# Groups of products kept together in TensorE's program

## The chip, the cores and the metric

The kernel runs on one core of a Trainium2 chip. The metric is the device time of one execution in microseconds; the median of 3 runs of the kernel before is 1662.76 us (1661.94 to 1663.72).

## The reference: what is computed

One inference step through two layers, for 128 context tokens and 256 latent tokens of width 2048, in fp32. Each layer starts with an RMSNorm that is shifted and scaled by a modulation vector, `silu(cond) @ mod_w + mod_b`, a product of a vector with a 2048 x 6144 matrix for each of two conditions (`c` for the latent, `c_ctx` for the context tokens).

- Layer 0: `proj = h @ w_in` (2048 x 6400). Part of it goes into a bidirectional RWKV-7 recurrence with 16 heads of 64, `s = s * w - (s @ kk) kka + v k`, `o = s @ r`, over each token sequence and in both directions; another part through `real(fft2)` over tokens and channels. Both are gated by `silu` of a further part, and multiplied by a 2048 x 2048 output matrix.
- Layer 1: grouped-query attention, 32 query heads on 8 key heads of 64, over a window of 128 and 128 cached context keys, with a sink logit per head in the softmax; a `silu` gate and a second output matrix.
- After each layer: RMSNorm, a gate from the modulation, and the residual.

It returns the tokens, the recurrence's final context states, and the context keys and values of layer 1.

## The kernel before

**Large products.** Activations and weights are split into a rounded high part and the rest (`hhi`, `hlo`; `whi`, `wlo`, made by ScalarE at L258 and VectorE at L259), and each product of a 128-row block is three products of the one-pass type (mm3, L398 to L400). proj_cm gives accumulators with channels in partitions and 384 tokens in columns; proj_tm with tokens in partitions. Weights come as units of 128 x 512, loaded by SyncE's queue into 2 and later 4 buffers, and cast up to 2 or 3 units ahead (Stream).

**Small products** are fp32, and the profile shows each as two records. A unit of the modulation vector (mod_unit, L322) is four products, one for each block of 128 weight rows, whose outputs of 32 rows each go to the four quarters of one accumulator, ps_mod. Their raw weights come in three ways: `mraw` at the start (blocks that layer 0 needs first), `rawf` in a lane of the RWKV stage (FILL_MODS, 7 blocks in halves of 256 columns, one buffer), and `raw` in the weight stream during the gates and the first output projection (PE_MODS, 2 blocks of 512 columns, four units each). Other blocks are summed by VectorE (mod_sums, L345).

The recurrence is done in chunks of 64 tokens. For one chunk of a pair of heads: ps_ba (L1026) and ps_sc (L1046) are products of keys and queries within chunks, ps_z (L1101, L1111) part of solving a triangular system, ps_v (L1149) transposes values, and the chain from chunk to chunk has ps_p1 (L1168), ps_y (L1176), ps_o (L1188 and L1208) and ps_s (L1195). They take half the array's rows, half its columns, or both, and the two heads `h` of a pair lie in different halves. In attention, `scores` makes the logits of two heads (L1479 to L1485), transpose_p transposes the softmax (L1515 to L1521), and ps_pv (L1442, L1444) multiplies it with the values, again with two heads in the two halves of the array's columns.

**What sets the order.** The code is traced lane by lane: weave asks, by a planner's costs in each `yield`, which lane goes on, and the traced instructions are numbered. The number is the priority: it counts up, and LEAD, BOOST and BACK shift it for some lanes and steps. A scheduler then puts each engine's program in a fixed order: of the instructions that are ready it takes the one with the lowest number. So a product that is traced right behind another one can come later in TensorE's program, with other lanes' products between. At run time an engine takes its program in order.

Of the kernel before, what the change touches and what calls it, by code (L numbers as in the profile page):

```python
# [20 lines left out]
KT = 16  # L21
TP, TS = 128, 256
# [14 lines left out]

BACK = 120
# [265 lines left out]
class K:  # L304
    def __init__(self, tc, A):
        self.tc, self.nc, self.A = tc, tc.nc, A


    def mod_unit(self, raw, layer, b, u, dst, c0=0):
# [10 lines left out]
        for i in range(4):  # L320
            kt = 4 * u + i
            nc.tensor.matmul(acc[32 * i:32 * i + 32, :n], self.silu[:, 2 * kt:2 * kt + 32], raw[:, n * i:n * i + n],  # L322
                             start=(u == 0), stop=(u == 3), skip_group_check=True)
# [6 lines left out]
        for m in range(nm):  # L330
            nc.tensor.matmul(ps[:, 2 * m:2 * m + 2], rows[:, 128 * m:128 * m + 128], self.sel, start=True, stop=True)
# [5 lines left out]
    def mod_sums(self, raw, i, layer, b, u):  # L337
# [12 lines left out]
        for g in range(4):  # L350
            nc.tensor.matmul(ps[32 * g:32 * g + 32, 0:8], self.sel32, self.dacc[:, :, g], start=True, stop=True)
# [43 lines left out]

    def mm3(self, out, lh, ll, rh, rl, start, stop):
        mm = self.nc.tensor.matmul
# [186 lines left out]
    def layer0_in(self, acts, first):  # L584
# [32 lines left out]
        for kt in range(KT):  # L617
            sq = ip.tile([128, T], F32, name="sq", tag="sq", bufs=2)
            nc.scalar.activation(sq, xT[:, kt], AF.Square)
            nc.tensor.matmul(ps[:, :T], ones, sq, start=(kt == 0), stop=(kt == KT - 1))  # L620
# [192 lines left out]
    def dft(self, fp, ch, dt, us, ys, y):  # L813
# [8 lines left out]
        for tt in range(3):  # L822
            ps = self.pw.tile([128, 512], F32, name="ps_f1", tag="pw")
            ts = slice(128 * tt, 128 * tt + 128)
            nc.tensor.matmul(ps[:, 0:129], us[0][:, ts], ch[:, 0:129], start=True, stop=False)
            nc.tensor.matmul(ps[:, 65:129], us[1][:, ts], ch[:, 129:193], start=False, stop=False)
            nc.tensor.matmul(ps[:, 129:257], us[1][:, ts], ch[:, 193:321], start=False, stop=True)
            nc.scalar.copy(ab[:, tt], ps[:, 0:257])
# [5 lines left out]
        for out, c0, n, q in ((ps[:, 0:194], 1, 128, 0), (ps[:, 194:388], 129, 128, 1), (px[0:1, 0:194], 0, 1, 0)):  # L834
            for tt in range(3):
                nc.tensor.matmul(out[:, cols[tt]], ab[:, tt, c0:c0 + n], tabs[tt][q],
                                 start=(tt == 0 and c0 != 129), stop=(tt == 2 and c0 != 1))
# [63 lines left out]
    def wkv_elem(self, j, st):  # L901
# [25 lines left out]
        nc.tensor.matmul(ps[:, :T], self.bd, sq, start=True, stop=True)  # L927
# [7 lines left out]
        for q, src, dst in ((0, self.wl, p), (1, self.al, tha)):  # L935
            yield 0.92, 0, 1.8
            ps = [self.pw.tile([128, 512], F32, name="ps_lo", tag="pw") for _ in range(2)]
            for d in range(2):
                nc.tensor.matmul(ps[d][:, :T], up[64 * d:64 * d + 64, q], src[64 * d:64 * d + 64, :],
# [39 lines left out]
        nc.tensor.matmul(ps[:, :T], self.bd, sq, start=True, stop=True)  # L979
# [30 lines left out]
    def wkv_lower(self, j, st):  # L1010
# [4 lines left out]
        for v0s in ((8, 0), (4,)):  # L1015
# [6 lines left out]
            for i in range(n):  # L1022
                v = v0s[i // 4] + i % 4
                for h in range(2):
                    hs = slice(64 * h, 64 * h + 64)
                    nc.tensor.matmul(ps[hs, 64 * i:64 * i + 64], BK[hs, v, 0], A[hs, v], start=True, stop=True)  # L1026
# [6 lines left out]
    def wkv_score(self, j, st):  # L1033
# [3 lines left out]
        for v0 in (8, 0, 4):  # L1037
# [4 lines left out]
            for i in range(4):  # L1042
                for h in range(2):
                    hs = slice(64 * h, 64 * h + 64)
                    lh = BK[hs, v0 + i].rearrange("p a t -> p (a t)")
                    nc.tensor.matmul(ps[h][:, 128 * i:128 * i + 128], lh, AR[hs, :, v0 + i], start=True, stop=True)  # L1046
# [8 lines left out]
        for v0, n in ((0, 4), (4, 2), (8, 4)):  # L1055
            yield 0.22 * n, 0, 0.9
            ps = self.pw.tile([128, 512], F32, name="ps_bt", tag="pw")
            for i in range(n):
                nc.tensor.transpose(ps[:, 128 * i:128 * i + 128], BK[:, v0 + i].rearrange("p a t -> p (a t)"),
                                    self.ident)  # L1060
# [3 lines left out]
    def wkv_solve(self, p):  # L1064
# [31 lines left out]
        for u0, n in ((0, 16), (16, 8)):  # L1096
            yield 0.06 * n, 0, 0.5
            ps = self.pw.tile([128, 512], F32, name="ps_z", tag="pw")
            for u in range(n):
                for h in range(2):  # L1100
                    nc.tensor.matmul(ps[quad[2 * h + 1], 32 * u:32 * u + 32], TI[quad[2 * h], u0 + u, 32:64],  # L1101
                                     R[quad[2 * h], u0 + u, :], start=True, stop=True)
# [3 lines left out]
        for u0, n in ((0, 16), (16, 8)):  # L1106
            yield 0.06 * n, 0, 0.9
            ps = self.pw.tile([128, 512], F32, name="ps_z2", tag="pw")
            for u in range(n):
                for h in range(2):  # L1110
                    nc.tensor.matmul(ps[quad[2 * h], 32 * u:32 * u + 32], Z[quad[2 * h + 1], u0 + u, :],  # L1111
                                     DB[quad[2 * h + 1], u0 + u, :], start=True, stop=True)
# [5 lines left out]
    def wkv_chain(self, j, st):  # L1118

        nc, kp = self.nc, self.kp  # L1120
        TT, mm = nc.vector.tensor_tensor, nc.tensor.matmul
# [22 lines left out]
        def values(c):  # L1144

            ps = self.pw.tile([128, 512], F32, name="ps_v", tag="pw")
            for slot, s, d, _ in units(c):
                w0 = 64 * c + (TP if s == 0 else 0)
                mm(ps[64:128, 128 * slot:128 * slot + 128], (vrev if d else v)[:, w0:w0 + 64], self.ident,  # L1149
                   start=True, stop=True)  # L1150
# [10 lines left out]
        for c in range(4):  # L1161
# [4 lines left out]
            for slot, s, d, v_ in un:  # L1166
                for h in range(2):
                    mm(p1[64 * h:64 * h + 64, 64 * slot:64 * slot + 64], SC[:, 12 * h + v_, 0:64],  # L1168
                       SV[:, h, slot, :], start=True, stop=True)
# [3 lines left out]
            for slot, s, d, v_ in un:  # L1173
                for h in range(2):
                    hs, sl = slice(64 * h, 64 * h + 64), slice(64 * slot, 64 * slot + 64)
                    mm(yps[hs, sl], TI[hs, self.pos(v_)], P1[hs, sl], start=True, stop=True)  # L1176
# [8 lines left out]
            for slot, s, d, v_ in un:  # L1185
                for h in range(2):
                    hs, sl = slice(64 * h, 64 * h + 64), slice(64 * slot, 64 * slot + 64)
                    mm(ops[hs, sl], SB[hs, slot], R[hs, v_], start=(slot == 0), stop=False, skip_group_check=True)  # L1188
            if c < 3:
                yield 0.13 * ns, 0.7, 2.2  # L1190
                sps = self.pw.tile([128, 512], F32, name="ps_s", tag="pw")
                for slot, s, d, v_ in un:
                    for h in range(2):
                        q = (h * ns + slot) * 64
                        mm(sps[0:64, q:q + 64], BT[:, v_ - 2 * s, 64 * h:64 * h + 64], UV[:, h, slot, :],  # L1195
                           start=True, stop=True)
# [8 lines left out]
            for slot, s, d, v_ in un:  # L1205
                sl = slice(64 * slot, 64 * slot + 64)
                for h in range(2):
                    mm(ops[64 * h:64 * h + 64, sl], UV[:, h, slot, :], SC[:, 12 * h + v_, 64:128],  # L1208
                       start=False, stop=(slot == ns - 1), skip_group_check=True)
# [19 lines left out]
    def wkv_norm(self, j, st):  # L1229
# [6 lines left out]
        nc.tensor.matmul(ps[:, :T], self.bd, o, start=True, stop=True)  # L1236
# [5 lines left out]
        nc.tensor.matmul(ps[:, :T], self.bd, s2, start=True, stop=True)  # L1242
# [8 lines left out]
    def out_proj(self, layer, ys):  # L1251
# [10 lines left out]
        for b in range(4):  # L1262
# [3 lines left out]
            for m in range(4):  # L1266
                nc.tensor.matmul(ps[0:2, 128 * m:128 * m + 128], mc[:, g0 + b, m], self.ident, start=True, stop=True)
# [53 lines left out]
        if layer == 0:  # L1321
# [6 lines left out]
            for kt in range(KT):  # L1328
                ps = self.pw.tile([128, 512], F32, name="ps_t", tag="pw")
                for tt in range(3):  # L1330
                    nc.tensor.transpose(ps[:, 128 * tt:128 * tt + 128], xr[:, tt, 128 * kt:128 * kt + 128], self.ident)
# [12 lines left out]
    def layer1_mix(self, acts):  # L1344
# [78 lines left out]
        def heads(b):  # L1423
            for i in range(2):
# [13 lines left out]
                for kt in range(-1, 3):  # L1438
                    for hh in range(2):
                        hr = slice(64 * hh, 64 * hh + 64)  # L1440
                        if kt < 0:
                            nc.tensor.matmul(pv[hr, 0:TP], vp[:, gs], ps[hh][:, 768:896], start=True, stop=False)  # L1442
                        else:
                            nc.tensor.matmul(pv[hr, TP:T], vs[:, kt, gs], ps[hh][:, 256 * kt:256 * kt + 256],  # L1444
                                             start=False, stop=(kt == 2))
# [22 lines left out]
    def scores(self, qs, kh, kl, cmask):  # L1468
# [3 lines left out]
        mm = self.nc.tensor.matmul  # L1472
# [4 lines left out]
        for q, s in zip(qs, out):  # L1477
            for n, sc, qc, kc in jobs:
                mm(s[n][:, sc], q[:, qc], kh[:, kc], start=(sc.start == 0), stop=False)  # L1479
            mm(s[0][:, 128:256], cmask[:, 0:128], cmask[:, 128:256], start=False, stop=False)  # L1480
            mm(s[1][:, 0:128], cmask[:, 0:128], cmask[:, 256:384], start=False, stop=False)
        for j, (n, sc, qc, kc) in enumerate(jobs):
            for hh, (q, s) in enumerate(zip(qs, out)):
                hr = slice(64 * hh, 64 * hh + 64)
                mm(s[n][:, sc], q[hr, qc], kl[hr, kc], start=False, stop=(j > 0))  # L1485
# [23 lines left out]
    def transpose_p(self, ap, p):  # L1509
# [3 lines left out]
        for kt in range(2):  # L1513
            for qb in range(2):
                nc.tensor.transpose(ta[:, 256 * kt + 128 * qb:256 * kt + 128 * qb + 128],  # L1515
                                    p[qb][:, 128 * kt:128 * kt + 128], self.ident)
        nc.scalar.copy(PT[:, 0:512], ta)
        tb = self.pw.tile([128, 512], F32, name="ps_tb", tag="pw")
        for qb in range(2):
            nc.tensor.transpose(tb[:, 128 * qb:128 * qb + 128], p[qb][:, 256:384], self.ident)  # L1520
        nc.tensor.transpose(tb[:, 256:384], p[2], self.ident)  # L1521
# [19 lines left out]
```

## Time and profile before

| | before |
|---|---|
| median of 3 runs | 1662.76 us |
| the profiled execution | 1660.11 us, of which its span 1658.3 us |
| busy TensorE / VectorE / ScalarE | 1570.1 / 1072.3 / 811.3 us |
| mean granted TensorE clock | 0.979 |
| the large products into acc, L398 / L399 / L400, 1376 each | busy 479.6 / 473.9 / 473.6 us |
| ps_mod (L322), records, and busy: rawf, mraw, raw | 448, 256, 64; 53.0, 35.9, 28.2 us |
| chain that ended last: TensorE, VectorE, DMA, ScalarE | 72, 11, 9, 5% |

Busy is the time in which at least one instruction of a group ran; products overlap each other in TensorE, so durations of single ones add up to more. The stages along the span, as the lines that run in them show: modulation and first norm to about 130 us, RWKV to 640 us, Fourier mixing and gates to 895 us, the first output projection to 1035 us, the second norm and keys and values to 1110 us, attention to 1400 us, then its gates and the second output projection.

### The profile page before, as it was taken

To read this page: it belongs to the slowest core of one execution; us is meant where nothing else is said; L and a number is where in the kernel's file an instruction comes from. 1 tells how busy PE (TensorE), PEld (TensorE's weight loads), DVE (VectorE), ACT (ScalarE), POOL (GpSimd) and SP (SyncE) were. 2 spreads that over 40 slices of the span, in tenths; PEclk is the share of its full clock that TensorE was granted. 3 is DMA by queue.
4 is the path that set the end of the run, shared out by engine and by line. 5 is a ranking of instruction groups with operands and counts; after the bars stand their busy time and mean duration, and the time that the engine had idled before them with its cause. 6 is when DMAs were issued, how large, how long until landed. Compare 5 with 4: busy or idle time off the path is not lost.

```text
span 1658.3 us, 30019 instructions
## 1 busy us (share of the span) xinstructions
PE 1570.1 (95%) x11488; PEld 1296.5 (78%) x11488; DVE 1072.3 (65%) x2584; ACT 811.3 (49%) x1771; POOL 3.9 (0%) x21
## 2 busy tenths in 40 slices
PE   6899999999989989999999999899999999999998
PEld 2557678777777768889897777788888888998777
DVE  1326886587777585475664573899877999644344
ACT  3326656665667654354333333754555555333332
POOL 0000000000000000000000000000000000000000
PEclk8899999999999999999999999899999999999999
DMA  9975342253233243354456663567322334446443
GB/s 368 370 279 167 115 143 74 86 162 121 79 118 111 76 132 94 109 168 121 156 184 231 245 209 120 198 187 248 107 72 69 102 127 148 131 121 226 132 126 134
DMA packets 120247, 255.75 MB, mean 154 GB/s; under 512 B 12324, under 2 KB 45220, under 8 KB 109732
## 3 DMA queue, kind: packets, MB, share of 16 engines
q1 hardware_dynamic: 111528, 235.97, 43.3%
q10 hardware_dynamic: 8576, 17.86, 3.1%
q8 instruction: 90, 1.47, 0.4%
q14 instruction: 53, 0.43, 0.1%
HBM read 246.40 MB, written 7.39 MB: 153 GB/s over the span
## 4 chain that ended last, share of the span: by engine, by line
PE 72%; DVE 11%; DMA 9%; ACT 5%; issue 2%; ACTq 0%; SPq 0%; DVEq 0%
PE acc L398 11%; PE acc L399 11%; PE acc L400 11%; PE ps_mod L322 6%; DMA rawf<-modw 6%; PE acct L398 5%; PE acct L399 5%; PE acct L400 5%; DVE wlo L259 2%; DMA raw<-we 2%; DVE junk L345 1%; PE ps_pv L1444 1%; PE ps_v L1149 1%; PE ps_s L1195 1%; PE ps_y L1176 1%
## 5 line engine op out<-in xcount | busy, mean ns | idle before, releaser
L258 ACT CAST whi<-raw 128x512 fp32r<-128x512 f32 x480 | 295.5, 620 | 477.3 <-PE acc L399 207.6
L259 DVE TENSOR_TENSOR wlo<-raw,whi 128x512 fp32r<-128x512 f32 x480 | 327.9, 689 | 304.4 <-ACT whi L258 301.3
L398 PE MATMUL acc<-hhi,whi 128*128 128x384 f32 x1376 | 479.6, 349 | 13.9 <-ACT whi L258 7.2
L400 PE MATMUL acc<-hhi,wlo 128*128 128x384 f32 x1376 | 473.6, 345 | 0.8 <-DVE wlo L259 0.5
L399 PE MATMUL acc<-hlo,whi 128*128 128x384 f32 x1376 | 473.9, 344 | 0.0
L398 PEld LDWEIGHTS acc<-hhi,whi 128*128 128x128 f32 x1376 | 261.9, 190 | 48.9 <-issue 19.9
L399 PEld LDWEIGHTS acc<-hlo,whi 128*128 128x128 f32 x1376 | 262.6, 191 | 16.8 <-issue 15.4
L400 PEld LDWEIGHTS acc<-hhi,wlo 128*128 128x128 f32 x1376 | 262.0, 190 | 14.2 <-issue 9.6
L345 DVE SCALAR_TENSOR_TENSOR junk<-raw,srow 128x512 f32<-128x512 f32 x224 | 154.2, 688 | 5.8 <-DMA raw<-modw 2.4
L398 PE MATMUL acct<-whi,yhi 128*128 128x512 f32 (+1 forms) x432 | 154.8, 360 | 1.2 <-DVE yb L1276 0.9
L399 PE MATMUL acct<-wlo,yhi 128*128 128x512 f32 (+1 forms) x432 | 154.7, 358 | 0.8 <-DVE wlo L259 0.8
L400 PE MATMUL acct<-whi,ylo 128*128 128x512 f32 (+1 forms) x432 | 154.3, 358 | 0.0
L398 PEld LDWEIGHTS acct<-whi,yhi 128*128 128x128 f32 x432 | 81.5, 189 | 21.6 <-DVE yb L1276 5.3
L399 PEld LDWEIGHTS acct<-wlo,yhi 128*128 128x128 f32 x432 | 81.5, 189 | 17.4 <-issue 4.2
L400 PEld LDWEIGHTS acct<-whi,ylo 128*128 128x128 f32 x432 | 81.5, 189 | 16.5 <-issue 4.4
L322 PE MATMUL ps_mod<-rawf,silu 128*32 128x256 f32 x448 | 53.0, 404 | 23.1 <-DMA rawf<-modw 23.1
L322 PE MATMUL ps_mod<-mraw,silu 128*32 128x512 f32 x256 | 35.9, 667 | 10.9 <-DMA mraw<-modw 10.9
L322 PEld LDWEIGHTS ps_mod<-rawf,silu 128*32 128x32 f32 x448 | 12.4, 109 | 41.5 <-DMA rawf<-modw 25.4
L327 ACT COPY mrow<-ps_mod 128x256 f32<-128x256 f32 (+1 forms) x24 | 11.1, 461 | 63.1 <-PE ps_mod L322 63.1
L1086 DVE TENSOR_TENSOR work<-work 128x30 f32<-128x30 f32 (+14 forms) x120 | 39.3, 328 | 1.9
L1084 DVE TENSOR_TENSOR work<-work 128x30 f32<-128x30 f32 (+14 forms) x120 | 39.3, 327 | 1.9
L1494 DVE TENSOR_REDUCE ast<-ps_sa 128x1 f32<-128x384 f32 x64 | 25.4, 416 | 19.2 <-PE ps_sa L1485 19.1
(298 smaller groups left out, 2169.8 us busy)
## 6 DMA issues: line engine op xcount, KB each, us to landing
raw<-we SPq DMA_DIRECT2D x200, 256.0 KB, 2.8
raw<-wo SPq DMA_DIRECT2D x160, 256.0 KB, 2.7
raw<-modw SPq DMA_DIRECT2D x36, 1024.0 KB, 5.7
mraw<-modw SPq DMA_DIRECT2D x32, 1024.0 KB, 8.2
rawf<-modw SPq DMA_DIRECT2D x56, 512.0 KB, 3.9
raw<-weo SPq DMA_DIRECT2D x64, 256.0 KB, 2.8
raw<-woo SPq DMA_DIRECT2D x64, 256.0 KB, 2.7
G<-gd ACTq DMA_DIRECT2D x4, 1024.0 KB, 6.9
```

Source lines behind the costliest of these rows:

```text
L258: k.nc.scalar.copy(hi, raw)
L259: k.nc.vector.tensor_tensor(lo, raw, hi, op=ALU.subtract)
L322: nc.tensor.matmul(acc[32 * i:32 * i + 32, :n], self.silu[:, 2 * kt:2 * kt + 32], raw[:, n * i:n * i + n], start=(u == 0), stop=(u == 3), ...
L345: nc.vector.scalar_tensor_tensor(junk, raw[:, 512 * i:512 * i + 512], 1.0, self.srow[:, c], op0=ALU.mult, op1=ALU.mult, accum_out=self.dac ...
L398: mm(out, lh, rh, start=start, stop=False)
L399: mm(out, lh, rl, start=False, stop=False)
L400: mm(out, ll, rh, start=False, stop=stop)
L1084: TT(tv, X[:, s + 1:32, s:s + 1].to_broadcast([128, n, s]), X[:, s:s + 1, 0:s].to_broadcast([128, n, s]), op=ALU.mult)
L1086: TT(X[:, s + 1:32, 0:s], X[:, s + 1:32, 0:s], tv, op=ALU.add)
L1149: mm(ps[64:128, 128 * slot:128 * slot + 128], (vrev if d else v)[:, w0:w0 + 64], self.ident, start=True, stop=True)
L1176: mm(yps[hs, sl], TI[hs, self.pos(v_)], P1[hs, sl], start=True, stop=True)
L1494: nc.vector.tensor_reduce(st[:, 0, i:i + 1], src[i], axis=AX.X, op=ALU.max)
```

## The change

Inside `with self.together():` the first product that is traced is the head. Each later one of the block gets an order edge that puts it behind the head (`issue_after`, an edge without a semaphore), and a priority that is better by 1,000,000. Every product goes through `mm` or `tp`; outside such a block these do what the direct calls did. The blocks are: a unit of ps_mod, ps_mt, the first Fourier products, ps_ba, ps_sc, ps_bt, ps_z, ps_v, ps_p1, ps_y, both halves of ps_o, ps_s, ps_pv, the scores of two heads, and each of the two groups of transposes. In some, the order within the block is changed too: ps_o, ps_s and ps_pv start with head h = 1, ps_sc counts down, ps_ba runs through the indices as `x ^ 3`, ps_ta and ps_tb start with another block.

```
+NEXT = 1000000
+    def on_pe(self, op, args, kw):
+        if self.head is None:
+            op(*args, **kw)
+        elif not self.head:
+            self.head.append(op(*args, **kw).ins)
+        else:
+            with self.tc.issue_after(self.head[0]):
+                self.tc.cur_priority -= NEXT
+                op(*args, **kw)
+                self.tc.cur_priority += NEXT
+
+    def mm(self, *args, **kw):
+        self.on_pe(self.nc.tensor.matmul, args, kw)
+
+    def tp(self, *args, **kw):
+        self.on_pe(self.nc.tensor.transpose, args, kw)
+
+    @contextmanager
+    def together(self):
+
+        self.head = []
+        yield
+        self.head = None
...
 (mod_unit)
-        for i in range(4):
-            kt = 4 * u + i
-            nc.tensor.matmul(acc[32 * i:32 * i + 32, :n], self.silu[:, 2 * kt:2 * kt + 32], raw[:, n * i:n * i + n],
+        with self.together():
+            for i in range(4):
+                kt = 4 * u + i
+                self.mm(acc[32 * i:32 * i + 32, :n], self.silu[:, 2 * kt:2 * kt + 32], raw[:, n * i:n * i + n],
...
 (wkv_chain, ps_s; ps_v, ps_p1, ps_y, ps_o alike)
-                for slot, s, d, v_ in un:
-                    for h in range(2):
-                        q = (h * ns + slot) * 64
-                        mm(sps[0:64, q:q + 64], BT[:, v_ - 2 * s, 64 * h:64 * h + 64], UV[:, h, slot, :],
+                with self.together():
+                    for slot, s, d, v_ in un:
+                        for h in (1, 0):
+                            q = (h * ns + slot) * 64
+                            mm(sps[0:64, q:q + 64], BT[:, v_ - 2 * s, 64 * h:64 * h + 64], UV[:, h, slot, :],
...
 (heads, ps_pv)
-                for kt in range(-1, 3):
-                    for hh in range(2):
+                with self.together():
+                    for kt in range(-1, 3):
+                        for hh in (1, 0):
...
 (transpose_p, ps_tb)
-        for qb in range(2):
-            nc.tensor.transpose(tb[:, 128 * qb:128 * qb + 128], p[qb][:, 256:384], self.ident)
-        nc.tensor.transpose(tb[:, 256:384], p[2], self.ident)
+        with self.together():
+            self.tp(tb[:, 256:384], p[2], self.ident)
+            for qb in range(2):
+                self.tp(tb[:, 128 * qb:128 * qb + 128], p[qb][:, 256:384], self.ident)
```

## Rows read from the trace of the kernel before

**Rows 1.** Busy time by stage: bounds, length, each engine's busy us, clock, DMA, GB/s.
```profile
130.00:640.00 510.00, 477.07 (x4804) 376.46 (x4803) 370.46 (x931) 316.01 (x667) 2.58 (x12) 0.98 0.37 116
800.00:1035.00 235.00, 233.58 (x1177) 185.11 (x1176) 133.10 (x289) 77.58 (x147) 0.00 (x0) 1.00 0.58 197
1110.00:1400.00 290.00, 284.04 (x1770) 247.89 (x1770) 252.65 (x721) 156.53 (x414) 0.00 (x0) 0.99 0.39 125
```

**Rows 2.** The chain of waits, 800 to 1035 us: shares, then two pieces.
```profile
by line: PE acct L398 14.6%; PE acct L399 14.2%; PE acct L400 14.2%; PE acc L398 10.8%; PE ps_mod L322 10.8%; PE acc L399 10.6%; PE acc L400 10.5%; DVE junk L345 3.8%; DMA raw<-modw 3.0%; DVE wlo L259 1.8%; issue 1.6%; PE ps_mg L1267 1.5%; 
...
804.02 0.99 PE ps_mod L322 x6
...
1028.82 0.98 PE ps_mod L322 x2
```

**Rows 3.** TensorE in order of time, around one whole unit: start, length, instruction.
```profile
82.44 0.33 PE L399 MATMUL acc<-hlo,whi 128*128 128x384 f32 x1
82.61 0.34 PE L400 MATMUL acc<-hhi,wlo 128*128 128x384 f32 x1
82.88 1.07 PE L322 MATMUL ps_mod<-mraw,silu 128*32 128x512 f32 x8
83.87 0.45 PE L398 MATMUL acc<-hhi,whi 128*128 128x384 f32 x1
```

**Rows 4.** TensorE in order of time, around a unit of 512 columns in parts.
```profile
826.54 0.34 PE L398 MATMUL acc<-hhi,whi 128*128 128x384 f32 x1
826.72 0.34 PE L399 MATMUL acc<-hlo,whi 128*128 128x384 f32 x1
826.90 0.33 PE L400 MATMUL acc<-hhi,wlo 128*128 128x384 f32 x1
827.16 1.04 PE L322 MATMUL ps_mod<-raw,silu 128*32 128x512 f32 x2
828.14 0.44 PE L398 MATMUL acc<-hhi,whi 128*128 128x384 f32 x1
...
829.48 0.45 PE L399 MATMUL acc<-hlo,whi 128*128 128x384 f32 x1
```

**Rows 5.** TensorE in order of time, around a whole unit of 256 columns.
```profile
362.79 0.34 PE L398 MATMUL acc<-hhi,whi 128*128 128x384 f32 x1
363.06 0.64 PE L322 MATMUL ps_mod<-rawf,silu 128*32 128x256 f32 x8
363.63 0.44 PE L399 MATMUL acc<-hlo,whi 128*128 128x384 f32 x1
```

**Rows 6.** TensorE in order of time, around a unit of 256 columns in parts.
```profile
213.97 0.34 PE L398 MATMUL acc<-hhi,whi 128*128 128x384 f32 x1
214.24 0.62 PE L322 MATMUL ps_mod<-rawf,silu 128*32 128x256 f32 x2
214.78 0.45 PE L399 MATMUL acc<-hlo,whi 128*128 128x384 f32 x1
...
215.71 0.44 PE L400 MATMUL acc<-hhi,wlo 128*128 128x384 f32 x1
```

**Rows 7.** Waits, 800 to 1035 us: who waited for whom, us, times, longest.
```profile
ACT whi L258 <- PE acct L400: 67.9, 39, 5.0
```

**Rows 8.** TensorE in order of time: ps_s and ps_v of one chunk.
```profile
561.95 0.32 PE L1149 MATMUL ps_v<-cmat,v 128*64 128x128 f32 x1
562.01 0.28 PE L1195 MATMUL ps_s<-work,BT 128*64 128x64 f32 x2
```

**Rows 9.** Waits of TensorE, 130 to 640 us.
```profile
PE ps_mod L322 <- DMA rawf<-modw: 23.1, 21, 4.1
```

**Rows 10.** TensorE in order of time: ps_pv of two heads, scores between.
```profile
1246.97 0.43 PE L1442 MATMUL ps_pv<-PT,vpr 128*64 128x128 f32 x2
1247.33 0.51 PE L1479 MATMUL ps_sa<-kh,q 128*128 128x384 f32 x2
...
1248.41 0.32 PE L1442 MATMUL ps_pv<-PT,vpr 128*64 128x128 f32 x1
```

More of the change, by code (lines that the diff above doesn't have):

```diff
@@ L1 @@
 import math
-from contextlib import ExitStack
+from contextlib import ExitStack, contextmanager
 from itertools import chain
@@ L1041, in wkv_score @@
             ps = [self.pw.tile([128, 512], F32, name="ps_sc", tag="pw") for _ in range(2)]
[L1042 to L1046, printed above, removed]
+            with self.together():
+                for i in (3, 2, 1, 0):
+                    for h in range(2):
+                        hs = slice(64 * h, 64 * h + 64)
+                        lh = BK[hs, v0 + i].rearrange("p a t -> p (a t)")
+                        self.mm(ps[h][:, 128 * i:128 * i + 128], lh, AR[hs, :, v0 + i], start=True, stop=True)
             for h in range(2):
@@ L1098, in wkv_solve @@
             ps = self.pw.tile([128, 512], F32, name="ps_z", tag="pw")
[L1099 to L1102, printed above, removed]
+            with self.together():
+                for u in range(n):
+                    for h in range(2):
+                        self.mm(ps[quad[2 * h + 1], 32 * u:32 * u + 32], TI[quad[2 * h], u0 + u, 32:64],
+                                         R[quad[2 * h], u0 + u, :], start=True, stop=True)
             for h in range(2):
@@ L1108, in wkv_solve @@
             ps = self.pw.tile([128, 512], F32, name="ps_z2", tag="pw")
[L1109 to L1112, printed above, removed]
+            with self.together():
+                for u in range(n):
+                    for h in range(2):
+                        self.mm(ps[quad[2 * h], 32 * u:32 * u + 32], Z[quad[2 * h + 1], u0 + u, :],
+                                         DB[quad[2 * h + 1], u0 + u, :], start=True, stop=True)
             for h in range(2):
@@ L1146, in values @@
             ps = self.pw.tile([128, 512], F32, name="ps_v", tag="pw")
[L1147 to L1150, printed above, removed]
+            with self.together():
+                for slot, s, d, _ in units(c):
+                    w0 = 64 * c + (TP if s == 0 else 0)
+                    mm(ps[64:128, 128 * slot:128 * slot + 128], (vrev if d else v)[:, w0:w0 + 64], self.ident,
+                       start=True, stop=True)
             ns = len(units(c))
@@ L1172, in wkv_chain @@
             yps = self.pw.tile([128, 512], F32, name="ps_y", tag="pw")
[L1173 to L1176, printed above, removed]
+            with self.together():
+                for slot, s, d, v_ in un:
+                    for h in range(2):
+                        hs, sl = slice(64 * h, 64 * h + 64), slice(64 * slot, 64 * slot + 64)
+                        mm(yps[hs, sl], TI[hs, self.pos(v_)], P1[hs, sl], start=True, stop=True)
             for h in range(2):
@@ L1184, in wkv_chain @@
             ops = self.pw.tile([128, 512], F32, name="ps_o", tag="pw")
[L1185 to L1188, printed above, removed]
+            with self.together():
+                for slot, s, d, v_ in un:
+                    for h in (1, 0):
+                        hs, sl = slice(64 * h, 64 * h + 64), slice(64 * slot, 64 * slot + 64)
+                        mm(ops[hs, sl], SB[hs, slot], R[hs, v_], start=(slot == 0), stop=False, skip_group_check=True)
             if c < 3:
@@ L1204, in wkv_chain @@
             yield 0.13 * ns, 0.3, 0.7
[L1205 to L1209, printed above, removed]
+            with self.together():
+                for slot, s, d, v_ in un:
+                    sl = slice(64 * slot, 64 * slot + 64)
+                    for h in (1, 0):
+                        mm(ops[64 * h:64 * h + 64, sl], UV[:, h, slot, :], SC[:, 12 * h + v_, 64:128],
+                           start=False, stop=(slot == ns - 1), skip_group_check=True)
             if c < 3:
```

111 lines of the change are left out of this document (60 added, 51 removed).

## The prediction, made before the result was known

> **What bounds the kernel now.** I read the busy time by stage first, then the chain of waits, then TensorE's own sequence in time order. TensorE is busy for 477 of 510 us in the RWKV stage (130 to 640 us), 233.6 of 235 us from the gates to the end of the first output projection (800 to 1035 us) and 284 of 290 us in attention [rows 1]; VectorE is busy for 370, 133 and 253 us there. So in the second of these stages nothing but TensorE's work sets the time, in attention VectorE is close behind, and in the RWKV stage TensorE has small holes. The first 130 us wait for weights and hold no group that is cut; between 640 and 800 us, and after 1400 us, TensorE's sequence has hardly a group in parts.
>
> The point is what that busy time is made of. In the middle stage ps_mod alone is 10.8% of the chain of waits, in 26 pieces of about 0.98 us (804.02 the first, 1028.82 the last) [rows 2]. These belong to 8 units (two column blocks, PE_MODS, of four units) of four products each; a 27th run, at 926.34, is not on the chain. A unit is 8 records, because an fp32 product is two, so 8 units would be 8 runs.
>
> What a cut costs is read from starts. Projection products follow each other at 0.17 us (82.44, 82.61). A unit of 8 between two of them moves the next one from 82.61 to 83.87: 1.26 - 0.17 = 1.09 us for four products [rows 3]. One product alone moves it from 826.90 to 828.14: 1.24 - 0.17 = 1.07 us, and in alternation from 828.14 to 829.48: 1.34 - 0.17 = 1.17 us [rows 4]. So a lone product costs what the four cost together: the four use 32 columns each, run side by side, and a cut throws that away. With 256 columns it is the same: held 363.63 - 362.79 - 0.17 = 0.67 us [rows 5], alone 0.64 us (213.97 to 214.78), in alternation 0.76 us (214.78 to 215.71) [rows 6].
>
> The alternation is strictly one to one, projection, ps_mod, projection, ps_mod. That is what counted priorities give: each traced instruction has the next number, and a unit set back by BACK (or ahead by the lane's lead) has the same numbers as the projection products of another place. It is no lack of data, since the next product is ready: TensorE starts it as soon as it is free.
>
> **The change part by part.** No product, copy or DMA is added or removed; products change their order in TensorE's program, and a few groups start with another member. So every term is TensorE time, and the question is how much of it comes out at the end.
>
> *Does the hold take?* The followers depend on the head by an order edge alone, without a semaphore. The projections show how such an edge behaves: L398, L399 and L400 add into one accumulator, and each must stay behind the one before. A gate projection of 256 columns has two accumulators, so at 826.54 the other one's product is ready as well, yet L399 and L400 follow L398 at 0.18 us with nothing between [rows 4]. So a follower is free as soon as its head is issued, and with 1,000,000 better it goes next. I cost the followers at no wait: they read the same weights or tiles that were ready with the head, or, where h runs (1, 0), operands that were written before the head's.
>
> *ps_mod, 512 columns, 800 to 1035 us.* 27 runs at a mean of 1.12 us (between 1.07 and 1.17) are 30.2 us; 8 held units at 1.09 us are 8.7 us. TensorE gets 21.5 us back. What is late next: in this stage ScalarE's casts wait for TensorE, 67.9 us on the output projection's products alone [rows 7], so the weights are there early, and VectorE has 100 us to spare. DMA engines are busy for 0.58 of the stage and would be for 0.58 x 235 / 214 = 0.64. But 3.0% of the chain is a DMA of mod weights, 3.8% VectorE's mod sums and 1.8% wlo, about 20 us that may grow a little [rows 2]. I take 0.9 of 21.5: **-19 us**. Ends: -21.5 and -12 (the 20 us grow by half).
>
> *ps_mod, 256 columns, 130 to 640 us.* 56 units (FILL_MODS: 7 blocks, two halves, four units each) stand in 82 runs, counted over the stage: 41 are whole, and the other 15 units lie in 41 runs, as 2+6 or 2+2+2+2. 26 runs too many at 0.64 to 0.76, mean 0.72 us: 18.7 us of TensorE time. In the same stage the score products (L1046) stand in 37 runs for 24 groups, mostly cut by these very runs, so their re-entry is in the 0.72. The chain's products (L1168 to L1208) are nearly whole already: I take -2 us for them. Against it, ps_v (L1149) writes the upper 64 columns and ps_s the lower; where they alternate now they run side by side, 561.95 over 562.01 [rows 8]. Held, each ps_v group of up to 4 products may lose up to 0.2 us, 32 groups: 0 to +6 us; I take +2, since most of ps_s is done before the first ps_v starts. TensorE time: -18.7 - 2 + 2, about -19 us. Here TensorE has holes of 33 us, of which 23.1 us are ps_mod waiting for its own DMA [rows 9]: one buffer, reloaded after each unit, so a faster stage meets that DMA earlier. Part of the gain becomes this wait or the chain's own latency over ScalarE and VectorE. I take 0.6: **-11 us**. Ends: -23 and +4.
>
> *Attention, 1110 to 1400 us.* ps_pv's first product goes alone before the second head's transposes are done: 0.36 us (1246.97 to 1247.33) and some 0.09 us for going in, while its partner later also runs alone (1248.41) [rows 10]. Whole, the group goes in and out once. About 0.40 us x 16 = 6.4 us of TensorE time. VectorE is at 253 of 290 us and the softmax is a chain through it, so I take half: **-3 us**. Ends: -6.4 and +3 (scores held as 16 products delay the transposes behind them by up to a microsecond, of 16 times perhaps 3 on the path).
>
> *The rest* (transposes, ps_ba, ps_z, ps_mt, the Fourier products): same array shape as their neighbours, or whole already; 0, ends -3 and +2.
>
> Sum: -19 - 11 - 3 = **-33 us** against the profiled execution's 1660.1 us, 1627 us. The median of the runs shown is 2.65 us above that execution, so 1630 us.
>
> A rule that speaks against this: the Trainium skill (TensorE: Matmul & The Clock Gate, Part 3, "What overlaps and what doesn't") says a weight load overlaps running products only where the row group differs. ps_mod's four products share all 128 rows, so by it they would go one after another, held or not, and a cut would cost only going in and out. The trace disagrees: eight records end 1.07 us after the first starts, two 1.04 us [rows 3, 4]. By the rule some 45 runs too many at about 0.2 us would give -9 us in place of -40; an estimate from the page that I don't use.
>
> **The rivals.**
> 1. *Only the middle stage pays.* The RWKV stage is set by its chain and its DMA, attention by VectorE, and their holes grow by what TensorE saves. For it: the 23.1 us at rawf [rows 9]. Against: holes of 33 us in 510 leave most of that stage to TensorE. Time: 1662.8 - 19 = 1644 us.
> 2. *All TensorE time comes out.* 21.5 + 19 + 6.4 = 47 us: 1616 us. For it: TensorE is never idle for lack of work in the middle stage, and a group that ends sooner also releases its chain sooner. Against: the holes above.
> 3. *The hold is one slot late, and it gets slower.* If a follower is free only after one more product has gone, every group becomes head, stranger, rest. The 56 units then make 112 runs, +30 x 0.72 = +22 us; the 8 make 16, -11 x 1.12 = -12 us; 24 score groups +11 runs at 0.7, +8 us; about 100 of the chain's groups at 0.3 us, +30 us. Together +48 us of TensorE time, at half in the RWKV stage about +18 us: 1681 us. It decides from the point where more than 40 of the groups that are whole now get cut. Against it: the unbroken triples.
> 4. *Held groups stand in front of the chain.* TensorE takes its program in order, so a chain product that comes ready behind a held score group waits up to a microsecond. To cancel 33 us it needs some 40 such waits on the path, of 24 score groups and 56 units. Time: about 1660 us, no change.
>
> **How the numbers follow.** A difference of 0.2%, 3.3 us, is about what a measurement of this kernel can tell from none. Chances: the forecast 0.58 (its own range 1620 to 1639), rival 1 0.18 (1639 to 1652), rival 2 0.12 (1608 to 1620), rival 3 0.06, rival 4 and unforeseen reorderings 0.06. Faster: 0.58 + 0.18 + 0.12, with a little of the last, 0.89; same 0.04; slower 0.07. The range runs from 1612, inside rival 2, to 1650, inside rival 1; what is left out is rivals 3 and 4 and the far ends.
>
> **What would show it.** ps_mod in runs of 8 throughout: 8 on the chain in the middle stage where 26 stood, none of x2; that stage's ps_mod busy time down from 28 us to about 9. The stage up to the first output projection's end 19 us shorter, the RWKV stage about 11. ps_pv in runs of 16. Wrong would be: runs of x2 still there (rival 3), or TensorE's busy time down by 40 us with the span down by less than 20 (rival 1), new waits of TensorE on VectorE in attention, or longer waits at rawf.

## The result and the profile after

The changed kernel takes 1603.9 us (median of 4 runs, 1596.4 to 1605.5) against 1662.4 us for the kernel before: a ratio of 0.964, 95% interval 0.961 to 0.967, 58 us less. I forecast 1630 us with a range from 1612 to 1650; the way was right, the gain was nearly twice as large, and the time lies outside the range. Two later sets of runs of it, on two chips, gave 1603.8 and 1603.1 us. Single executions of one kernel differ here by up to 1%: the first profiled one took 1596.4 us, the fastest of its four, and a second one (called *again* below) 1602.3 us. Where a size matters I use the second.

Cut at the first product of each stage, from the start and lengths of TensorE's instructions in us:

| stage, from the first product of one kind to that of the next | before | after | again | again less before | forecast |
|---|---|---|---|---|---|
| start, to rawf's first unit | 135.5 | 135.9 | 135.5 | 0.0 | 0 |
| RWKV, to the first Fourier product | 598.2 | 565.7 | 568.6 | -29.6 | -11 |
| Fourier products, to the last one | 53.0 | 52.7 | 52.8 | -0.2 | 0 |
| gates and first output projection, to ps_t | 259.3 | 236.7 | 238.9 | -20.4 | -19 |
| norm, keys, values, to the first scores | 108.0 | 107.0 | 107.9 | -0.1 | 0 |
| attention, to the last ps_pv | 243.3 | 241.5 | 241.6 | -1.7 | -3, with the next |
| the rest | 252.7 | 246.8 | 247.0 | -5.7 | |

The rest is counted to the start of TensorE's last product. The last two rows belong together: the lane of projections that runs beside attention is further on when the last ps_pv is done, with 587 records into acc left behind it where 619 were left before. The RWKV row ends at the first Fourier product, 733.7 us in the kernel before, not at the prediction's 640 us.

First, TensorE in order of time in the middle stage of the kernel after. L406 is a group's head, L410 a follower, L404 a product outside any group.

```profile
771.28 0.34 PE L404 MATMUL acc<-hhi,wlo 128*128 128x384 f32 x1
771.55 0.62 PE L406 MATMUL ps_mod<-raw,silu 128*32 128x512 f32 x1
771.55 0.63 PE L410 MATMUL ps_mod<-raw,silu 128*32 128x512 f32 x3
772.00 0.59 PE L406 MATMUL ps_mod<-raw,silu 128*32 128x512 f32 x1
772.01 0.60 PE L410 MATMUL ps_mod<-raw,silu 128*32 128x512 f32 x3
772.54 0.44 PE L404 MATMUL acc<-hhi,whi 128*128 128x384 f32 x1
```

The four products of a unit start together, and the next projection product comes 1.26 us after the last: exactly the whole unit of [rows 3], where [rows 4] had a lone product at each place. So the hold takes. It takes all 8 units of this stage and 55 of the 56 in the RWKV stage. The one exception (from 245.31 us in *again*) has its head, then 62 records of a ps_z group, then its followers: the head of ps_z had been taken just before it, and a head has no better priority of its own.

The chain of waits, 754 to 992 us of the kernel after, shares and two of its pieces:

```profile
by line: PE acct L404 40.1%; PE acc L404 35.0%; DMA raw<-modw 7.2%; PE ps_mod L406 2.8%; DMA raw<-weo 2.6%; issue 2.2%; DVE junk L350 2.1%; DVE wlo L261 2.0%; DVE yb L1347 1.1%; ACT osq L1351 0.9%; ACT L1382 0.5%; DVE xr L1359 0.5%; DVE yb 
...
771.62 0.55 PE ps_mod L406
...
793.66 0.55 PE ps_mod L406
```

ps_mod had 10.8% of this chain [rows 2] and has 2.8%. The DMA of mod weights has 7.2% in place of 3.0%, so something of what I feared for this stage did come, but it costs little: busy time shows that TensorE has hardly a hole there.

Busy time over the RWKV and the middle stage, cut as in the table (bounds, length, TensorE's busy us first). Before:

```profile
135.50:733.70 598.20, 561.02 (x5774) 449.68 (x5775) 416.05 (x1026) 360.42 (x768) 2.58 (x12) 0.98 0.38 118
786.80:1046.10 259.30, 257.33 (x1337) 208.49 (x1335) 145.93 (x317) 90.75 (x181) 0.00 (x0) 1.00 0.55 187
```

The changed kernel, again:

```profile
135.50:704.10 568.60, 533.81 (x5775) 437.85 (x5776) 416.12 (x1029) 360.45 (x768) 2.56 (x12) 0.98 0.40 125
756.90:995.80 238.90, 236.24 (x1337) 207.04 (x1336) 145.79 (x317) 90.85 (x182) 0.00 (x0) 0.99 0.60 203
```

This is the reading that decides the case. Subtract busy from length: TensorE's holes in the RWKV stage were 598.2 - 561.0 = 37.2 us and are 34.8 us; in the middle stage 2.0 and 2.7 us. Busy time fell by 27.2 and 21.1 us, length by 29.6 and 20.4. What TensorE's program lost, the time lost, about one to one; the holes hardly changed. The granted clock is 0.98 in both profiles of the RWKV stage, and 1.00 and 0.99 in those of the middle stage, so it is not the clock that made the difference. The wait on which I had built the discount stayed too, 19.8 us where [rows 9] had 23.1:

```profile
PE ps_mod L406 <- DMA rawf<-modw: 19.8, 18, 4.0
```

### The profile page after: what moved, and what is told of

It reads as the page before. It is cut to its first block, busy times and chain, and to the rows that moved or that the text cites. A ratio compares the mean times of both kernels' runs of the same rounds, so it can differ in the third digit from the quotient of the medians.

```text
span 1594.6 us, 30005 instructions
## 1 busy us (share of the span) xinstructions
PE 1507.3 (95%) x11488; PEld 1275.6 (80%) x11488; DVE 1069.1 (67%) x2584; ACT 810.9 (51%) x1771; POOL 3.9 (0%) x21
## 4 chain that ended last, share of the span: by engine, by line
PE 64%; DVE 16%; DMA 11%; ACT 6%; issue 3%; ACTq 0%; DVEq 0%; SPq 0%
PE acc L404 31%; PE acct L404 16%; DMA rawf<-modw 5%; DVE wlo L261 3%; PE ps_mod L406 3%; DVE junk L350 2%; DMA raw<-we 2%; DMA mraw<-modw 1%; DMA raw<-modw 1%; PE ps_o L410 1%; PE ps_v L410 1%; PE ps_pv L410 1%; ACT whi L260 1%; PE ps_s L410 1%; PE ps_sa L410 1%
## 5 line engine op out<-in xcount | busy, mean ns | idle before, releaser
L404 PE MATMUL acc<-hhi,whi 128*128 128x384 f32 x1376 | 478.3, 348 | 12.5 <-ACT whi L260 5.7
L404 PE MATMUL acc<-hlo,whi 128*128 128x384 f32 x1376 | 472.9, 344 | 0.0
L404 PE MATMUL acc<-hhi,wlo 128*128 128x384 f32 x1376 | 470.7, 343 | 1.7 <-DVE wlo L261 1.3
L404 PEld LDWEIGHTS acc<-hhi,whi 128*128 128x128 f32 x1376 | 261.3, 190 | 44.2 <-issue 18.1
L404 PEld LDWEIGHTS acc<-hlo,whi 128*128 128x128 f32 x1376 | 261.3, 190 | 13.7 <-issue 11.9
L404 PEld LDWEIGHTS acc<-hhi,wlo 128*128 128x128 f32 x1376 | 260.9, 190 | 11.1 <-issue 5.5
L404 PE MATMUL acct<-whi,yhi 128*128 128x512 f32 (+1 forms) x432 | 154.4, 358 | 2.4 <-DVE yb L1318 2.1
L404 PE MATMUL acct<-wlo,yhi 128*128 128x512 f32 (+1 forms) x432 | 153.9, 356 | 0.0
L404 PE MATMUL acct<-whi,ylo 128*128 128x512 f32 (+1 forms) x432 | 153.7, 356 | 0.0
L404 PEld LDWEIGHTS acct<-whi,yhi 128*128 128x128 f32 x432 | 81.5, 189 | 20.7 <-DVE yb L1318 6.5
L404 PEld LDWEIGHTS acct<-whi,ylo 128*128 128x128 f32 x432 | 81.5, 189 | 12.4 <-issue 0.2
L404 PEld LDWEIGHTS acct<-wlo,yhi 128*128 128x128 f32 x432 | 81.5, 189 | 11.8
L406 PE MATMUL ps_mod<-rawf,silu 128*32 128x256 f32 x112 | 35.0, 395 | 22.5 <-DMA rawf<-modw 22.3
L406 PE MATMUL ps_mod<-mraw,silu 128*32 128x512 f32 x64 | 35.5, 668 | 9.7 <-DMA mraw<-modw 9.7
L1118 DVE TENSOR_TENSOR work<-work 128x30 f32<-128x30 f32 (+14 forms) x120 | 39.2, 327 | 2.1
L1120 DVE TENSOR_TENSOR work<-work 128x30 f32<-128x30 f32 (+14 forms) x120 | 39.2, 327 | 1.9
L1538 DVE TENSOR_REDUCE ast<-ps_sa 128x1 f32<-128x384 f32 x64 | 25.3, 415 | 20.3 <-PE ps_sa L410 20.1
L406 PEld LDWEIGHTS ps_mod<-rawf,silu 128*32 128x32 f32 x112 | 7.7, 108 | 36.2 <-DMA rawf<-modw 25.6
L410 PE MATMUL ps_mod<-rawf,silu 128*32 128x256 f32 x336 | 35.9, 395 | 0.0
```

Of the source, the lines that this page charges most:

```text
L404: op(*args, **kw)
L406: self.head.append(op(*args, **kw).ins)
L410: op(*args, **kw)
L1118: TT(tv, X[:, s + 1:32, s:s + 1].to_broadcast([128, n, s]), X[:, s:s + 1, 0:s].to_broadcast([128, n, s]), op=ALU.mult)
L1120: TT(X[:, s + 1:32, 0:s], X[:, s + 1:32, 0:s], tv, op=ALU.add)
L1538: nc.vector.tensor_reduce(st[:, 0, i:i + 1], src[i], axis=AX.X, op=ALU.max)
```

## The experiments

All medians stand beside runs of the kernel before on the same chip, which gave 1660.9 to 1662.1 us.

**again, again_2.** The changed kernel, unchanged. 

> The changed kernel once more, beside the next three on one chip. Both theories: about 1604 us, 58 us under the kernel before. Where its profiled execution took 1596 us, 6 to 9 us less than its other runs, a second profile shows whether the 32 us that the RWKV stage came out shorter there are typical: if the difference lies in that stage it will now be some 26 us shorter, if in the weight-bound first 130 us it stays at 32.

 

> The changed kernel beside them: 1604 us under both theories.

 Measured: 1603.8 us, ratio 0.966 (0.961 to 0.970), and 1603.1 us, 0.965 (0.962 to 0.967). The RWKV stage is 29.6 us shorter in the profile of *again* and 30.4 in that of *again_2*, neither 26 nor 32: part of the first profile's extra 6 us lay in that stage, part in the middle one.

**mod_only.** Holds a unit of ps_mod, nothing else (the inner orders stay as changed).

```
-    def together(self):
-        self.head = []
+    def together(self, on=True):
+        self.head = [] if on else None
...
-            with self.together():        (all groups but mod_unit's four products)
+            with self.together(False):
```

> Only the four products of a ps_mod unit are held; the other groups keep their new inner order but are not held. Counting TensorE's program with the rows' costs (0.095 us for a change of array shape, a product's own time otherwise, products on different parts of the array side by side), it is 45 us shorter than before's: 18 in the RWKV stage, 20 in the middle stage, 7 in attention, where the new inner order alone does it. Theory A (TensorE's program is what comes out, one to one): 1617 us. Theory B (whole groups of the chain also shorten the chain's waits, and that is the surplus of some 10 us in the RWKV stage): no surplus here, 1617 us with the RWKV stage 18 us shorter. Theory C (the surplus comes from ps_mod, whose lone products stood in front of chain products): 1607 us, with the RWKV stage 28 us shorter.

Measured: 1609.4 us, ratio 0.969 (0.965 to 0.973). RWKV stage 578.7 us, 19.5 less than before, with holes of 36.6 us:

```profile
136.00:714.70 578.70, 542.10 (x5774) 443.58 (x5775) 416.06 (x1026) 360.41 (x768) 2.57 (x12) 0.98 0.40 121
```

That is what I had worked out for ps_mod there as TensorE time, 18.7 us, without a discount. So by the stage theory C, with 28 us, falls, and so does my share of 0.6. By the median alone C's 1607 us would be nearer than A's 1617. The count behind A priced a cut by the change of shape alone; the prediction's own prices from [rows 3 to 6] (18.7 and 21.5 us, against 18 and 20) account for about 2 of the 8 us, and attention, at 8.9 us in place of 7, for another 2. The rest is not explained.

**all_but_mod.** The reverse: every group but ps_mod's. 

> All groups are held but ps_mod's. By the same count TensorE's program is 19 us shorter: 12 in the RWKV stage, none in the middle stage, 7 in attention. Theory A: 1643 us. Theory B (surplus from the chain's whole groups): 1633 us, RWKV stage 22 us shorter. Theory C: 1643 us. The middle stage (800 to 1035 us) must be as long as before under each.

 Measured: 1641.3 us, ratio 0.988 (0.985 to 0.992), RWKV stage 15.1 us shorter, middle stage 1.2 us longer in the one profile, about as long as before, as each theory had it. The median is at A's end. In the RWKV stage the two halves sum to 34.6 us and give 29.6 together, since a lone ps_mod product that cut a score group in two is counted in both: here ps_mod's own busy time in the stage falls from 53.0 to 48.2 us without being held, and in mod_only that of ps_sc from 34.5 to 32.8.

**zero_products.** Adds known TensorE work and nothing else.

```
             for i in range(4):
                 kt = 4 * u + i
                 self.mm(acc[32 * i:32 * i + 32, :n], self.silu[:, 2 * kt:2 * kt + 32], ...
+            for i in range(4 if n == 256 else 0):
+                self.mm(acc[32 * i:32 * i + 32, :n], self.silu[:, 32:64], raw[:, n * i:n * i + n], ...
```

> The changed kernel, and behind the four products of each of the 56 ps_mod units of the RWKV stage four more of the same size with a stationary operand of zeros, held in the same group: 24 us more of TensorE's time in that stage by the count, no new wait, the same result. Theory A (one to one): 24 us above the changed kernel. My prediction's share of 0.6: 14 us above it. If the stage were bound by its DMA and its chain: under 8 us.

Measured: 1624.1 us, 20.3 us above the changed kernel on the same chip.

```profile
136.10:726.00 589.90, 553.65 (x6222) 449.27 (x6223) 419.99 (x1026) 360.66 (x768) 2.57 (x12) 0.99 0.39 120
```

TensorE is busy for 19.8 us more than in *again* (533.8), the stage is 21.3 us longer, and the holes are 36.2 us. So added work comes out about one to one as well, up to what the executions differ by (the granted clock is 0.99 here and 0.98 in *again*); 0.6 of 24 would have been 14.

**order_only.** No group held, the new order inside groups kept (`together(False)` everywhere). 

> No group is held; only the new order inside the groups stands (ps_pv, ps_o and ps_s from head 1, ps_sc and ps_ba in another sequence, the transposes of ps_ta and ps_tb from another block). If attention's 7.5 us (1.7 up to the last ps_pv, 5.7 behind it) come from holding, as my prediction had it: no change, 1661 us. If they come from the new first member, which waits for the last operand, so that the rest finds all it needs: attention and what follows 7.5 us shorter, ps_pv in runs of 16 without any hold, 1653 us.

 Measured: 1654.2 us, ratio 0.995 (0.993 to 0.997). Up to the last ps_pv 1.8 us less, behind it 5.7 us less: all of attention's gain, and no gain elsewhere. TensorE in order of time shows what changed:

```profile
1250.94 0.44 PE L404 MATMUL ps_pv<-PT,vpr 128*64 128x128 f32 x4
1251.21 1.47 PE L404 MATMUL ps_pv<-PT,vs 128*64 128x256 f32 x12
1252.61 0.50 PE L404 MATMUL ps_sa<-kh,q 128*128 128x384 f32 x2
```

ps_pv is whole without any hold, and where [rows 10] had scores between, they now follow. Its first member now is the head whose transposes are traced last. The transposes' own order changed with it, and no run separates the two.

**sc_ba_only.** Holds ps_ba, ps_sc, ps_bt and ps_z only. 

> Held are ps_ba, ps_sc, ps_bt and ps_z alone; ps_mod and the chain are not. My prediction gave these nothing. Counting TensorE's program: 11 us less in the RWKV stage, since a lone ps_mod product that stood between two score products now stands outside, with 7.5 us in attention from the order alone. Theory A (TensorE's program, one to one): RWKV stage 11 us shorter, 1642 us. Theory B (the chain's whole groups): under 5 us there, 1650 us.

 Measured: 1639.6 us, ratio 0.988 (0.983 to 0.992), 14.6 us under order_only; RWKV stage 16.7 us shorter than before, with holes of 36.3 us.

```profile
136.40:717.90 581.50, 545.23 (x5775) 439.00 (x5776) 414.40 (x1026) 360.00 (x768) 2.58 (x12) 0.98 0.39 121
```

I had given these groups nothing, and the count behind the expectation had 11 us.

**chain_only.** Holds ps_v, ps_p1, ps_y, ps_o and ps_s only. 

> Held are the chain's groups alone (ps_v, ps_p1, ps_y, ps_o, ps_s). The count gives under 1 us in the RWKV stage. Theory A: as order_only, within 3 us. Theory B (whole groups shorten the chain's waits): the RWKV stage 8 to 10 us shorter than in order_only.

 Measured: 1649.3 us, ratio 0.994 (0.991 to 0.997), against order_only's 0.995 (0.993 to 0.997): the intervals lie on each other, and in one profile the RWKV stage is 2.0 us shorter than before and 4.2 us shorter than in order_only, between the two theories. By itself inconclusive within 5 us; no_chain says more.

**edge_only.** All edges, no better priority: `NEXT = 0`. 

> All groups have their order edge, and no follower a better priority (NEXT = 0). If the priority is what holds: groups as much in parts as in order_only, and its time within 3 us. If the edge alone keeps a group together: near the changed kernel's 1604 us.

 Measured: 1652.0 us, ratio 0.995 (0.992 to 0.998), as order_only. In the chain of waits of its middle stage (here 800 to 1035 us) ps_mod has 7.9 and 2.4% for followers and heads, where the changed kernel has 2.8% in all:

```profile
by line: PE acct L404 42.9%; PE acc L404 29.9%; PE ps_mod L410 7.9%; DVE junk L350 4.7%; DMA raw<-modw 2.9%; PE ps_mod L406 2.4%; issue 2.0%; DVE wlo L261 1.8%; PE ps_mg L404 1.5%; ACT osq L1351 1.0%; PE ps_mt L410 0.6%; DVE yb L1347 0.6%; 
```

The edge alone doesn't hold a group; with the better priority it does. Whether the priority would do it without the edge was not run.

In fact the edge alone left TensorE's sequence as it was: in order of time, TensorE's 11488 records of edge_only and order_only have the same tiles and shapes in the same sequence. So the two profiles show how far two executions of one TensorE program lie apart. The RWKV stage of order_only, then of edge_only:

```profile
135.50:735.90 600.40, 564.16 (x5774) 452.62 (x5775) 415.40 (x1027) 361.06 (x768) 2.57 (x12) 0.97 0.37 117
137.40:728.40 591.00, 554.11 (x5775) 442.11 (x5776) 415.50 (x1027) 360.56 (x768) 2.58 (x12) 0.99 0.38 119
```

The length differs by 9.4 us and busy time by 10.1, at granted clocks of 0.97 and 0.99; the holes are 36.2 and 36.9 us. A stage's length in one profile is thus good to a few us only where the clocks agree, as they do, at 0.98, in the RWKV stage of the kernel before, *again*, mod_only, all_but_mod, sc_ba_only, no_chain and wider_groups.

**no_chain.** Every group but the chain's. 

> All groups are held but the chain's (ps_v, ps_p1, ps_y, ps_o, ps_s). By the count of TensorE's program under 1 us more than the changed kernel. Theory A (TensorE's program, one to one; what ps_mod alone does not bring comes from ps_ba and ps_sc): as the changed kernel, within 3 us, 1604 us. Theory B (the chain's whole groups end sooner and shorten its waits): as mod_only, 1609 us.

 Measured: 1605.0 us, ratio 0.966 (0.964 to 0.969), 1.9 us above the changed kernel on the same chip. The interval (1600.5 to 1609.2 us) just reaches theory B's 1609; the RWKV stage decides for theory A, at 569.8 us where again_2 has 567.8 and mod_only 578.7:

```profile
138.90:708.70 569.80, 535.81 (x5776) 438.29 (x5777) 415.10 (x1026) 360.00 (x768) 2.56 (x12) 0.98 0.40 123
```

So the hold of the chain's groups is worth about 2 us, no more than executions differ by.

**wider_groups.** ps_md held too, and ps_s, the next ps_v and the second ps_o as one group.

```
-        for g in range(4):               (ps_md)
-            self.mm(ps[32 * g:32 * g + 32, 0:8], ...
+        with self.together():
+            for g in range(4):
+                self.mm(ps[32 * g:32 * g + 32, 0:8], ...
...
-            with self.together():          (ps_v and the second ps_o; ps_s starts the list so)
+            with self.together(head=so):
```

> The changed kernel, with two groups more held: the four products of ps_md (which stood singly, 32 columns each), and ps_s, the next chunk's ps_v and the second half of ps_o as one group (all of the shape 128x64, and all ready with the last of ps_y's copies). By the count of TensorE's program 3 to 3.5 us less than the changed kernel: 1600 us against 1604, of which this measurement can show little. Theory B (whole groups shorten the chain's waits) would give 8 us or more, in the RWKV stage.

 Measured: 1601.3 us, ratio 0.963 (0.961 to 0.965). In the profile the last stage is 2.4 us shorter than in *again*, where ps_md stood singly; the RWKV stage is as long, and the middle stage 3.3 us longer. About what the count says, and not told from nothing by the medians.

**fill_later_0, _60, _150.** The fill lane's lead of 100 set to 0, -60, -150, on top of wider_groups; the fourth expectation is for the repeat with 0.

```
-LEAD = (0, 0, 300, 300, 0, 0, 0, 0, 100)
+LEAD = (0, 0, 300, 300, 0, 0, 0, 0, 0)
```

> As wider_groups, and the lane of the 56 ps_mod units has a lead of 0 in place of 100, so that a unit is taken later and its DMA has landed more often when TensorE comes to it. The program costs the same by the count. My prediction took TensorE's wait at rawf (some 20 us) as something that eats gains; if it is simply a cost beside the others, less of it shows one to one: with the wait at 10 us, 10 us less than wider_groups. If another product then waits in its place: no change.

> As fill_later_0 with a lead of -60: the wait at rawf shorter again, under 8 us, and the RWKV stage by what the wait lost. The lane ends later in the stage; 242 projection products still stand behind its last unit, so it does not become the end of the stage.

> As fill_later_0 with a lead of -150. The wait at rawf near none, but the units now run behind more of the projection: 129 projection products fewer stand at the stage's end than in the others' order. If the chain is then left without cover at the end, slower than fill_later_60 by up to 10 us; if not, the fastest of the four.

> If the shorter wait at rawf is a gain: 1598 to 1599 us again, 5 us under the changed kernel. If the first result was the spread between executions: within 2 us of wider_groups, 1601 us.

Measured: 1598.6 and, repeated, 1596.6 us with a lead of 0 (ratio 0.961, 0.958 to 0.964, and 0.962, 0.959 to 0.964; 6.5 us under again_2 on its chip); 1604.4 us with -60 and 1615.7 us with -150 (0.972, 0.971 to 0.974). With 0, TensorE's wait at rawf is halved, here in the repeat:

```profile
PE ps_mod L407 <- DMA rawf<-modw: 8.6, 10, 1.7
```

Most of that does not come out. From the start of the span to the first Fourier product, a stretch in which these kernels and wider_groups have the same number of TensorE records to within one, the holes were 59.9 us in wider_groups and are 57.2 and 57.9 us. The wait is 9 and 11 us shorter, so 2 to 3 us of it show and my 10 us were too many: in the first of the two runs ps_mt now waits 3.8 us for its copy and ps_m 4.5 for ScalarE. The medians fell by 3 to 5 us.

With -60 the wait is 11.4 us and the holes of that stretch 58.1 us, about as with 0, but TensorE is busy in it for 649.5 us where the repeat with 0 has 640.0. The four executions with -60 had granted clocks of 0.972 to 0.978, the nine with 0 had 0.975 to 0.984, so its longer time is not shown to come from the waits. With -150 the clock was lower still (0.969 to 0.974); there the projection also waits for its casts, 6.1 and 5.0 us, and ps_mod for rawf 17.9 us.

I had expected gains down to -60 and saw none behind 0. The version with a lead of 0 is the fastest that I found, by its medians: its interval touches the changed kernel's.

## Why the prediction was wrong

**The mechanism: right.** The hold takes, ps_mod stands in runs of 8 but for one unit, its busy time in the middle stage is 8.5 us where 28.2 stood (I said about 9), ps_pv is whole.

**The middle stage: right.** -19 us forecast, -20.4 and -22.6 in two profiles; undiscounted it was 21.5.

**The RWKV stage: the term that failed.** -11 us forecast, with -23 as its far end; it is -29.6. Two numbers in it were mis-sized.

- *The share of 0.6.* I argued that part of the gain becomes a longer wait at rawf or the chain's own latency. mod_only shows 19.5 us where the undiscounted term was 18.7, zero_products the same in the other direction, and the holes stay between 33 and 37 us in every kernel with the fill lane's old lead (before 37.2, mod_only 36.6, sc_ba_only 36.3, zero_products 36.2, again 34.8, wider_groups 33.1), while busy time runs from 530 to 564 us. The holes were there and I counted them rightly; that they were there says nothing on whether they grow. By the prediction's own sum (0.4 of 18.7) this is worth 7.5 us.
- *The other groups at net nothing* (-2 for the chain, +2 for ps_v, 0 for the rest). They bring 5.6 us by the medians (1609.4 against 1603.8) and 10.1 us by the RWKV stage of the profiles. About 2 us of that are the chain's (no_chain), as I had them; the rest is, by elimination, that of ps_ba, ps_sc, ps_bt and ps_z, which bring 16.7 us when they alone are held (sc_ba_only), ps_mod's products that then no longer cut them included. I had put the score products' cuts into the price of the lone ps_mod product. That price was read where a lone product stood between two projection products, though; where a lone product stood in ps_sc, the score products themselves also lost their partner in the other half of the rows. The busy time of their tiles over the RWKV stage shows it. Before, ps_mod and then ps_sc:

```profile
135.50:733.70 598.20, 53.04 (x448) 12.44 (x448) 5.19 (x14) 0.98 0.38 118
...
135.50:733.70 598.20, 34.46 (x384) 27.64 (x384) 31.07 (x48) 0.98 0.38 118
```

The changed kernel, *again*, the same two:

```profile
135.50:704.10 568.60, 37.30 (x448) 9.10 (x448) 5.21 (x14) 0.98 0.40 125
...
135.50:704.10 568.60, 29.21 (x384) 24.98 (x384) 30.69 (x48) 0.98 0.40 125
```

ps_mod lost 15.7 us; ps_sc went from 34.5 to 29.2, ps_ba from 16.9 to 14.6, ps_o from 39.2 to 35.7, ps_bt from 13.9 to 12.7 and ps_s from 24.9 to 23.7, another 13.4 us, in the same two profiles. Together 29.1, and busy time as a whole fell by 27.2; tiles run at the same time, so the sum is a guide and not an account. Of these, ps_s's part and 2 us of ps_o's come with the new order alone (23.8 and 37.2 us in order_only). The loss that I allowed for ps_v did not come: 30.1 us before, 30.0 after.

**Attention: right in sign, half in size, wrong in what brings it.** -3 us forecast, -7.4 measured, undiscounted 6.4. ps_pv comes out whole, as I had it, but order_only shows that holding has no part in it: the new order does it. The discount for VectorE (253 us busy of 290) was wrong in the same way as the share above: TensorE's holes from the first scores to the last ps_pv were 2.3 us and are 3.0.

**The rivals.** Rival 1 (only the middle stage pays, 1644 us) fell with mod_only. Rival 2 (all TensorE time comes out, 1616 us, 0.12) was the right one, and short only by the other groups' 6 to 10 us and attention's last microsecond. Rival 3 fell with the first rows above, rival 4 with the result. The range's lower end was set inside rival 2 and had no room for a TensorE term that was itself too small.

The rule of the Trainium skill that I weighed (TensorE: Matmul & The Clock Gate, Part 3, "What overlaps and what doesn't") gave -9 us by my estimate. That the four products would go one after another was my step from it; the page's sentence is on weight loads. The measured 58 us, and whole units whose eight records end 1.07 us after the first starts [rows 3], leave no room for that step here.

## What to carry to other kernels

Here TensorE was busy for 94% of the stage, and what was saved on it or added to it came out about whole. In such a stage, do not discount a saving because there are holes; first look for something that shows that they will grow, and test it with known extra work. Count a cut group from both sides, what the intruder costs and what the group loses by being split. And see which member of a group is ready last: to issue that one first may hold the group together for nothing.

## What the runs showed of the hardware

Executions of one kernel spread by up to 1% (the kernel before 1653.9 to 1669.7 us over 23 runs), and the faster profiles have the higher mean granted clock: 0.984 at a span of 1594.6 us and 0.977 at 1600.5 us for the same program. I can't say from these runs what sets it. One profile a kernel was therefore good for holes, which lie within 1 us of each other for the one program of order_only and edge_only and within 2.2 us for three profiles of the changed kernel (35.6, 34.8 and 33.4), and for a stage's length only to a few us and at like clocks. The 0.2% that I had taken as the least difference to be told is less than this spread.
